# Two-layer fp32 encoder trunk on one core: FFN activations and x turned in 32x32 squares on VectorE and regrouped through scratch in device memory

## The chip, the cores and the metric

The kernel runs on one core of a Trainium2 chip. The core has five engines with a queue of instructions each: TensorE (PE; its weight loads are shown as PEld), VectorE (DVE), ScalarE (ACT), GpSimd (POOL) and SyncE (SP), and 16 DMA engines that move data between HBM and the core's own memory, SBUF. TensorE sums into PSUM. The metric is the device time of one execution in microseconds; the runs before have a median of 2511.64 us.

## The reference, cut to what matters

```python
for i in range(2):
    h = rms_norm(x, norm_mix_g[i])
    x = x + (retention_na_mixer if i == 0 else diff_attention_mixer)(h, ...)
    m = rms_norm(mem, norm_mem_g[i])
    x = x + memory_cross_attention(rms_norm(x, norm_xattn_g[i]), m, w_xq[i], w_xkv[i], w_xo[i], ...)
    x = x + swiglu_ffn(rms_norm(x, norm_ffn_g[i]), w_ffn_in[i], w_ffn_out[i])

def swiglu_ffn(h, w_in, w_out):
    g, u = jnp.split(h @ w_in, 2, axis=-1)
    return (jax.nn.silu(g) * u) @ w_out
```

x is 256 tokens x 2048 features, the FFN's hidden width is 5632, and everything is fp32.

## The kernel before

The 256 tokens are two tiles `t` of 128 rows; x stays in SBUF as `x_sb`, tokens on partitions. Every product with a weight matrix goes through `gemm`: the activation, features on partitions, is the stationary operand, the weight streams. Each fp32 number is held as two fp32r numbers, `hi` (a rounding copy) and `lo` (the remainder), and a product is three matmuls: hi x wh (L311), hi x wl (L312), lo x wh (L313).

Weights come in blocks of 512 x 512 fp32, 1 MB, into `raw` (three buffers) by SP's queue (L275). A block is used in two **units** of 256 rows. For a unit `prepare` has ScalarE cast `wh` (L285) and VectorE subtract `wl` (L286), three buffers each; `LOOK = 2` keeps two units prepared ahead, so the cast for unit n + 3 takes the buffer that unit n's matmuls read. A unit is 12 matmuls: three products, two rows of 128 features, two token tiles. There are 864 units. A block of 512 output columns sums over its units in two PSUM accumulators `acc` and ends with its epilogue.

The order of weights is a plan: per layer the mixer's input and output projections, the memory's key projection, xq, the memory's value projection, xo (the cross-attention's output projection), then the FFN in three groups of 4, 4 and 3 hidden blocks. For each group the gate and up columns are computed (`ffn_in`, two column blocks of eight units for each hidden block), and the group's part of the down product (`ffn_out`) follows. `woven` starts two column blocks of a phase on the features that are ready first and adds the last features later.

Work beside the matmuls is written as generators that a `Side` object steps once per unit. Each becomes instructions at that place in the program, and every engine runs its own instructions in that order.

What a matmul needs as stationary operand must stand with features on partitions, while x and the gated FFN activation `sg` stand with tokens there. `turn` (L335) turns 128x128 squares on TensorE by a matmul with the identity, four to a PSUM tile `pt`. `feed` uses it for the norms' inputs: two calls per 512 columns of `x_sb`, from which `gained` makes hi on ScalarE with the norm's gain (L340) and lo on VectorE (L341); the results are `hTx` for the cross-attention, `hTf` for the FFN and `hT` for the second layer's mixer. The norm's root over tokens is applied later, on the outputs: `finish_rstd` needs all four blocks' sums of squares and POOL's power. `act_T` does the same for the FFN's `sg`: two turns, then hi by `split` on ScalarE (L385) and lo on VectorE (L386), into `aT`. The queries and keys of the attention heads (`z`), retention's gate and the softmax tiles use `turn` or the like as well.

`add_x` (L697) adds a finished block to `x_sb`; L804 makes `sg` from the up accumulator.

Of the kernel before, what the change touches and what calls it, by code (L numbers as in the profile page):

```python
# [80 lines left out]
def trunk_kernel(  # L81
# [18 lines left out]
    qk = pool("qk", 1)  # L100
    vp = pool("vp", 2)
# [52 lines left out]
    def gain(i, layer, k):  # L154
        c = i * 32 + layer * 16 + k
        return gcol[:, c:c + 1]
# [58 lines left out]
    side = Side()  # L215
# [24 lines left out]
    for layer in range(2):  # L240
        j = layer // 2
# [10 lines left out]
        for g0, g1 in FFN_GROUPS:  # L252
            n = 2 * (g1 - g0)
# [72 lines left out]
    def square_sum(dst, src):  # L326
        junk = sqp.tile([P, NB], F32, tag="sq", name="junk")
        nc.scalar.activation(junk, src, AF.Square, accum_out=dst)

    def turn(srcs, u):  # L330
        pt = ps_t.tile([P, 2, T], F32, tag="pt", name="pt")
        for j in range(2):
            for t in range(2):
                c = (2 * u + j) * P
                nc.tensor.transpose(pt[:, j, t * P:(t + 1) * P], srcs[t][:, c:c + P], ident)  # L335
        return pt

    def gained(dst, kt, src, g):
        hi, lo = dst[0][:, kt], dst[1][:, kt]
        nc.scalar.activation(hi, src, AF.Copy, scale=g)  # L340
        nc.vector.scalar_tensor_tensor(out=lo, in0=src, scalar=g, in1=hi.bitcast(F32),  # L341
                                       op0=ALU.mult, op1=ALU.subtract)
# [20 lines left out]
    def finished(tasks):  # L363
        tasks = list(tasks)
        return lambda: all(t["done"] for t in tasks)

    def feed(dst, b, u, srcs, gi, layer, ssr, then=None):
        pt = turn(srcs, u)
        for j in range(2):
            k = 4 * b + 2 * u + j  # L370
            gained(dst, k, pt[:, j], gain(gi, layer, k))
        square_sum(ssr[0][:, u, b:b + 1], srcs[u])
        if then:
            then()
        return
        yield

    def feed_x(dst, b, gi, layer, ssr, wait=0):

        then = (lambda: finish_rstd(ssr)) if b == 3 else None  # L380
        t0 = side.add(feed(dst, b, 0, x_block(b), gi, layer, ssr), wait)
        return [t0, side.add(feed(dst, b, 1, x_block(b), gi, layer, ssr, then), wait + 1, finished([t0]))]

    def split(hi, lo, src):
        nc.scalar.copy(hi, src)  # L385
        nc.vector.tensor_sub(lo, src, hi)  # L386
# [299 lines left out]
    def finish_rstd(ssr):  # L686
        ss, rstd, r2 = ssr
        nc.vector.tensor_reduce(r2, ss, axis=AX.X, op=ALU.add)
        rsqrt_mean(rstd, r2, D)
        nc.vector.tensor_mul(r2, rstd, rstd)  # L690

    def x_block(b):
        return [x_sb[:, t, b * NB:(b + 1) * NB] for t in range(2)]
# [7 lines left out]
    hT = pair(which[0], "hT")  # L701
    ssr = new_ss("ssx")
# [12 lines left out]
    for layer in range(2):  # L715
        j = layer // 2
        A, B = which
        oT = pair(B, "oT")
        if layer % 2 == 0:
            gate = retention_na(j, hT, ssr[1:], oT, gate)  # L720
            kts = (8, 12, 0, 4)
        else:
            nc.vector.scalar_tensor_tensor(out=tabs, in0=tdiff, scalar=-1.0, in1=tdiff, op0=ALU.mult, op1=ALU.max)
            gate = diff_attention(j, hT, ssr[1:], oT, gate)
            kts = KT4

        mT = pair(A, "mT")
        m_v = mem[0].rearrange("(t p) d -> p t d", p=P)

        def mem_block(b):  # L730
            if layer == 0:
                mb = [att.tile([P, NB], F32, tag="att", name="mb") for _ in range(2)]
                for t in range(2):
                    nc.sync.dma_start(mb[t], m_v[:, t, b * NB:(b + 1) * NB])
            mts = [att.tile([P, 2, T], F32, tag="att", name="mt") for _ in range(2)]
            for u in range(2):
                nc.sync.dma_start(mts[u], mem_t[:, 4 * b + 2 * u:4 * b + 2 * u + 2])
            yield 2
            for u in range(2):
                feed_turned(mT, 2 * b + u, mts[u], 2, layer)  # L740
                yield 1
            if layer == 0:
                if b == 3:
                    side.drain(mtasks[:3])
                yield from block_sums(mb, b, mssr)

        mtasks = [side.add(mem_block(b)) for b in range(4)]

        gemm(kts, oT, lambda b, acc: add_x(acc, b), gate=gate)
        side.drain(mtasks)  # L750
        hT = pair(B, "hTx")
        ssr = new_ss("ssx")
        tasks = [t for b in range(4) for t in feed_x(hT, b, 1, layer, ssr, 1 if b == 3 else 0)]

        g = {"wait": 3}

        def epi_k(b, acc):
            g["k"], g["tk"] = normed_T(acc, mssr[1:], c_xk + layer, "kT")

        def epi_q(b, acc):  # L760
            g["q"], g["tq"] = normed_T(acc, ssr[1:], c_xq + layer, "qT")

        def epi_v(b, acc):
            g["v"] = tokens(acc, mssr[1:])

        gemm(KT4, mT, epi_k)
        gemm(KT4, hT, epi_q, gate=by_unit(tasks))
        xo = m8.tile([P, 2, 4, T], F32R, tag="m8", name="xo")
        xo = (xo[:, 0], xo[:, 1])
        heads = [side.add(attend(g, h, xo, h), cond=prepared(g)) for h in range(4)]  # L770
        gemm(KT4, mT, epi_v, steps=2)
        hT = pair(B, "hTf")
        ssr = new_ss("ssx")
        tasks = []

        def epi_xo(b, acc):
            add_x(acc, b)
            tasks.extend(feed_x(hT, b, 3, layer, ssr, 2))

        gemm((0,), xo, epi_xo, gate={0: heads[:2], 1: heads[2:]}, steps=2)  # L780
        gate = by_unit(tasks)

        def act_T(aT, zs, kt):
            for u in range(2):
                pt = turn(zs, u)
                split(aT[0][:, kt + 2 * u:kt + 2 * u + 2], aT[1][:, kt + 2 * u:kt + 2 * u + 2], pt)
                if u == 0:
                    yield 0

        for g0, g1 in FFN_GROUPS:  # L790
            aT = pair(A, "aT")
            n = g1 - g0
            sgs, atasks = {}, []

            def epi_in(i, acc):
                blk = i // 2
                r1 = ssr[1]
                if i % 2 == 0:
                    sgs[blk] = [zp.tile([P, NB], F32, tag="z", name="sg") for _ in range(2)]
                    for t in range(2):  # L800
                        nc.scalar.activation(sgs[blk][t], acc[t], AF.Silu, scale=r1[:, t:t + 1])
                    return
                for t in range(2):
                    nc.vector.scalar_tensor_tensor(out=sgs[blk][t], in0=acc[t], scalar=r1[:, t:t + 1],  # L804
                                                   in1=sgs[blk][t], op0=ALU.mult, op1=ALU.mult)
                atasks.append(side.add(act_T(aT, sgs[blk], 4 * blk), 2))

            gemm(KT4, hT, epi_in, gate=gate)
            gate = None
            kts = tuple(4 * b for b in range(n))  # L810
            last = g1 == 11
            side.drain(atasks[:-1])
            if last and layer == 0:
                hN = pair(B, "hT")
                ssn = new_ss("ssx")
                tasks = []

            def epi_out(b, acc):
                add_x(acc, b)
                if last and layer == 0:  # L820
                    tasks.extend(feed_x(hN, b, 0, 1, ssn, 1))
                elif last:
                    for t, xb in enumerate(x_block(b)):
                        nc.scalar.dma_start(out[0][t * P:(t + 1) * P, b * NB:(b + 1) * NB], xb)

            gemm(kts, aT, epi_out, gate={2 * n - 2: atasks[-1:]})
        if layer == 0:
            hT, ssr = hN, ssn
            gate = by_unit(tasks)
        which = which[::-1]  # L830
# [34 lines left out]
```

## Time and profile before

| what | value |
|---|---|
| three runs, median (range) | 2511.64 us (2511.25 to 2511.86) |
| the profiled execution, its own time | 2511.57 us |
| its span in the trace | 2509.8 us |
| TensorE busy | 2493.7 us, 99% |
| VectorE, ScalarE busy | 1427.0 us (57%), 1187.0 us (47%) |
| POOL busy | 50.6 us (2%) |
| HBM read, written | 465.91 MB, 2.10 MB |
| share of TensorE in the chain that ended last | 97% |

The span is the stretch that the trace covers. Matmuls are pipelined: the duration of one is longer than its distance to the next, so a stream is measured from start to start. The chain is followed back from the last instruction to whatever released it; an engine with a high share of busy time matters only where the chain runs through it. In a row of a timeline the bracket at the end is the idle time of the engine just before, and what ended it.

### The profile page before, as it was taken

How to read it: one execution, taken by the hardware profiler on the slowest of the kernel's cores; microseconds unless marked ns; L12 is line 12 of the kernel's file. 1: busy time of each engine (PE TensorE's matmuls, PEld its weight loads, DVE VectorE, ACT ScalarE, POOL GpSimd, SP SyncE). 2: the span in 40 equal slices, each digit the busy share in tenths (PEclk: the TensorE clock that was granted, in tenths of full speed). 3: DMA queues.
4: the chain of work that ended last, by engine and by line, in shares of the span. 5: the costliest groups of instructions: out<-in, count | busy, mean ns of one | idle time of the engine just before them, and what ended most of it. 6: DMA issues, size and time to landing. Idle time of an engine off the chain costs nothing.

```text
span 2509.8 us, 28710 instructions
## 1 busy us (share of the span) xinstructions
PE 2493.7 (99%) x11504; PEld 2067.5 (82%) x11504; DVE 1427.0 (57%) x1681; ACT 1187.0 (47%) x1538; POOL 50.6 (2%) x55
## 2 busy tenths in 40 slices
PE   8999999999999999999999999999999999999999
PEld 6888888888888888888888888888888888888887
DVE  6775565674545445544557766757654545455454
ACT  5554464564443444344445555645544444443443
POOL 1000000000000000000000000000000000000000
PEclk9999999999999999999999999999999999999999
DMA  8545566545555555555555555554555655556554
GB/s 285 183 159 182 186 220 200 168 163 190 186 189 195 188 197 185 190 196 185 185 185 167 168 169 179 199 190 155 183 184 188 197 186 196 189 185 200 186 189 163
DMA packets 236742, 469.87 MB, mean 187 GB/s; under 512 B 8128, under 2 KB 8768, under 8 KB 236608
## 3 DMA queue, kind: packets, MB, share of 16 engines
q1 hardware_dynamic: 233808, 463.50, 55.9%
q0 software_dynamic: 640, 2.10, 0.4%
q10 hardware_dynamic: 2160, 2.44, 0.3%
q8 instruction: 90, 1.47, 0.2%
q14 instruction: 44, 0.36, 0.0%
HBM read 465.91 MB, written 2.10 MB: 186 GB/s over the span
## 4 chain that ended last, share of the span: by engine, by line
PE 97%; DMA 1%; DVE 1%; ACT 0%; issue 0%; POOL 0%; ACTq 0%; DVEq 0%; POOLq 0%
PE acc L311 31%; PE acc L313 31%; PE acc L312 31%; PE pt L335 2%; DMA x_sb<-in_x 1%; PE pt L501 0%; PE pa_s L393 0%; PE pa_s L392 0%; PE pa_s L391 0%; PE pa_r L551 0%; DVE wl L286 0%; DMA dec<-in_ret_decay_bwd 0%; DMA lrow<-in_lambda_k 0%; PE pa_o L393 0%; PE pa_o L392 0%
## 5 line engine op out<-in xcount | busy, mean ns | idle before, releaser
L286 DVE TENSOR_TENSOR wl<-raw,wh 128x1024 fp32r<-128x1024 f32 (+1 forms) x865 | 1056.5, 1223 | 954.3 <-ACT wh L285 953.7
L285 ACT CAST wh<-raw 128x1024 fp32r<-128x1024 f32 (+1 forms) x865 | 910.3, 1052 | 1190.7 <-PE acc L313 1162.7
L311 PE MATMUL acc<-wh,hTfh 128*128 128x512 f32 x1408 | 551.5, 392 | 0.0
L313 PE MATMUL acc<-wh,hTfl 128*128 128x512 f32 x1408 | 548.5, 390 | 0.0
L312 PE MATMUL acc<-wl,hTfh 128*128 128x512 f32 x1408 | 547.9, 389 | 0.0
L311 PE MATMUL acc<-wh,hTh 128*128 128x512 f32 x832 | 331.9, 399 | 9.7 <-ACT wh L285 8.2
L312 PE MATMUL acc<-wl,hTh 128*128 128x512 f32 x832 | 325.6, 391 | 1.4 <-DVE wl L286 1.4
L313 PE MATMUL acc<-wh,hTl 128*128 128x512 f32 x832 | 325.6, 391 | 0.0
L313 PEld LDWEIGHTS acc<-wh,hTfl 128*128 128x128 f32 x1408 | 264.2, 188 | 55.6
L312 PEld LDWEIGHTS acc<-wl,hTfh 128*128 128x128 f32 x1408 | 264.4, 188 | 54.0
L311 PEld LDWEIGHTS acc<-wh,hTfh 128*128 128x128 f32 x1408 | 264.4, 188 | 53.8
L311 PE MATMUL acc<-wh,aTh 128*128 128x512 f32 x704 | 275.5, 391 | 0.0
L313 PE MATMUL acc<-wh,aTl 128*128 128x512 f32 x704 | 274.5, 390 | 0.0
L312 PE MATMUL acc<-wl,aTh 128*128 128x512 f32 x704 | 274.1, 389 | 0.0
L311 PEld LDWEIGHTS acc<-wh,hTh 128*128 128x128 f32 x832 | 156.9, 189 | 39.7 <-ACT wh L285 8.2
L313 PEld LDWEIGHTS acc<-wh,hTl 128*128 128x128 f32 x832 | 156.6, 188 | 33.8
L312 PEld LDWEIGHTS acc<-wl,hTh 128*128 128x128 f32 x832 | 157.0, 189 | 32.2 <-DVE wl L286 2.9
L313 PEld LDWEIGHTS acc<-wh,aTl 128*128 128x128 f32 x704 | 132.2, 188 | 27.7
L312 PEld LDWEIGHTS acc<-wl,aTh 128*128 128x128 f32 x704 | 132.2, 188 | 26.8
L311 PEld LDWEIGHTS acc<-wh,aTh 128*128 128x128 f32 x704 | 132.2, 188 | 26.9
L311 PE MATMUL acc<-wh,oTh 128*128 128x512 f32 x256 | 100.2, 391 | 0.0
L313 PE MATMUL acc<-wh,oTl 128*128 128x512 f32 x256 | 99.7, 390 | 0.0
(184 smaller groups left out, 1875.8 us busy)
## 6 DMA issues: line engine op xcount, KB each, us to landing
raw<-in_w_ffn_in SPq DMA_DIRECT2D x176, 1024.0 KB, 5.1
raw<-in_w_ffn_out SPq DMA_DIRECT2D x88, 1024.0 KB, 5.1
raw<-in_w_in_ab SPq DMA_DIRECT2D x55, 1024.0 KB, 5.2
raw<-in_w_in_c SPq DMA_DIRECT2D x48, 1024.0 KB, 5.2
raw<-in_w_out_ab SPq DMA_DIRECT2D x16, 1024.0 KB, 5.2
raw<-in_w_xkv SPq DMA_DIRECT2D x16, 1024.0 KB, 5.0
raw<-in_w_out_c SPq DMA_DIRECT2D x16, 1024.0 KB, 5.1
raw<-in_w_xq SPq DMA_DIRECT2D x8, 1024.0 KB, 5.2
```

Source lines behind the costliest of these rows:

```text
L285: nc.scalar.copy(wh[:, js], raw[:, rs])
L286: nc.vector.tensor_sub(wl[:, js], raw[:, rs], wh[:, js])
L311: nc.tensor.matmul(acc[t], lhsT=hi[:, kt, ts], rhs=wh[:, j], start=first and j == 0, stop=False)
L312: nc.tensor.matmul(acc[t], lhsT=hi[:, kt, ts], rhs=wl[:, j], start=False, stop=False)
L313: nc.tensor.matmul(acc[t], lhsT=lo[:, kt, ts], rhs=wh[:, j], start=False, stop=last and j == 1)
L335: nc.tensor.transpose(pt[:, j, t * P:(t + 1) * P], srcs[t][:, c:c + P], ident)
```

## The change

The turns of `x_sb` (for `hTx`, `hTf` and the second layer's `hT`) and of the FFN's `sg` leave TensorE. The new `regroup` takes both token tiles of a 512-column block: VectorE's transpose turns all 32x32 squares within their 32 partitions, one instruction per token tile, into a buffer `zt`; SP's queue writes the 512 KB to scratch in HBM (`zd`, four buffers); four loads on POOL's queue, one for each group of 32 features, bring the squares to the partitions that they belong to (`zT`). Five units later (`MOVE`) ScalarE and VectorE make hi and lo from `zT`, now from SBUF: in `feed` ScalarE four times 128x256 and VectorE eight times 128x128, in `act_T` two each over 128x4x128. The buffers are those of the heads' values (`vp`), of queries and keys (`qk`) and the single `m8`. `feed_x` adds one task instead of two.

```diff
+MOVE = 5
+    dram = pool("dram", 4, space=bass.MemoryType.DRAM)
-    def feed(dst, b, u, srcs, gi, layer, ssr, then=None):
-        pt = turn(srcs, u)
-        for j in range(2):
-            k = 4 * b + 2 * u + j
-            gained(dst, k, pt[:, j], gain(gi, layer, k))
-        square_sum(ssr[0][:, u, b:b + 1], srcs[u])
...
+    def regroup(srcs, room=""):
...
+        zt = zt.rearrange("p (j k t b) -> p j k t b", j=4, k=4, t=2)
+        for t in range(2):
+            nc.vector.transpose(zt[:, :, :, t], srcs[t].rearrange("p (k j a) -> p j k a", j=4, a=32))
+        zd = dram.tile([4, 32, 4, T], F32, name="zd")
+        nc.sync.dma_start(zd.rearrange("i a j n -> (i a) (j n)"), zt.rearrange("p j k t b -> p (j k t b)"))
+        for j in range(4):
+            nc.gpsimd.dma_start(zT[32 * j:32 * j + 32].rearrange("a (i n) -> a i n", i=4),
+                                zd[:, :, j].rearrange("i a n -> a i n"))
+        return zT.rearrange("p (i k t b) -> p i k t b", i=4, k=4, t=2)
+
+    def feed(dst, b, srcs, gi, layer, ssr, room):
+        zT = regroup(srcs, room)
+        for t in range(2):
+            square_sum(ssr[0][:, t, b:b + 1], srcs[t])
+        if b == 3:
+            finish_rstd(ssr)
+        yield MOVE
+        for k in range(4):
...
+            nc.scalar.activation(hi, src, AF.Copy, scale=g)
+            for t in range(2):
+                nc.vector.scalar_tensor_tensor(out=lo[:, t], in0=src[:, t], scalar=g, in1=hi[:, t].bitcast(F32),
+                                               op0=ALU.mult, op1=ALU.subtract)
...
         def act_T(aT, zs, kt):
-            for u in range(2):
-                pt = turn(zs, u)
-                split(aT[0][:, kt + 2 * u:kt + 2 * u + 2], aT[1][:, kt + 2 * u:kt + 2 * u + 2], pt)
-                if u == 0:
-                    yield 0
+            zT = regroup(zs)
+            yield MOVE
+            for t in range(2):
+                split(*(x[:, kt:kt + 4, t * P:(t + 1) * P].rearrange("p k (i b) -> p k i b", i=4) for x in aT),
+                      zT[:, :, :, t].rearrange("p i k b -> p k i b"))
...
-                atasks.append(side.add(act_T(aT, sgs[blk], 4 * blk), 2))
+                atasks.append(side.add(act_T(aT, sgs[blk], 4 * blk)))
```

The change moves instructions. Lines of the new kernel have other numbers: L287 is the cast, L288 the remainder, L313 to L315 the three matmuls, L381 the transpose, L383 the write, L385 the loads, L400 and L402 hi and lo of a feed, L411 the remainder of `act_T`, L722 the add to x, L829 the gate product. The numbers in the names count tiles; in the rows of the first two places they tell the units apart.

ScalarE where xo ends and the FFN begins, layer 0. Before: feeds 0 and 1 (`pt_4400`, then `pt_4431` and `pt_4442`) and the casts around them; `wh_4486` belongs to the first FFN unit:

```order
L285 CAST wh_4382<-raw_4362 128x1024
...
L340 ACTIVATE hTfh_4285<-pt_4400,gcol_104 128x256
L285 CAST wh_4415<-raw_4413 128x1024
L340 ACTIVATE hTfh_4285<-pt_4400,gcol_104 128x256
...
L285 CAST wh_4453<-raw_4413 128x1024
L340 ACTIVATE hTfh_4285<-pt_4431,gcol_104 128x256
L340 ACTIVATE hTfh_4285<-pt_4442,gcol_104 128x256
...
L285 CAST wh_4486<-raw_4484 128x1024
```

And now: the FFN's units 1 to 6 are `wh_4501`, `4517`, `4571`, `4599`, `4617` and `4645`, and the feeds 0, 1 and 2 are `zz_4400`, `zz_4432` and `zz_4484`:

```order
L287 CAST wh_4501<-raw_4499 128x1024
...
L287 CAST wh_4517<-raw_4499 128x1024
L287 CAST wh_4571<-raw_4569 128x1024
L400 ACTIVATE hTfh_4302<-zz_4400,gcol_106 128x256 x4
...
L287 CAST wh_4599<-raw_4569 128x1024
L287 CAST wh_4617<-raw_4615 128x1024
L400 ACTIVATE hTfh_4302<-zz_4432,gcol_106 128x256 x4
L287 CAST wh_4645<-raw_4615 128x1024
L400 ACTIVATE hTfh_4302<-zz_4484,gcol_106 128x256 x4
```

The copies of feed 0 have moved from before the first FFN unit's cast to behind that of unit 3, those of feed 1 behind that of unit 5.

VectorE at the same place, now: the adds of xo's last block (`acc0_4497`, `acc1_4498`), block 3's transposes (`zz_4547`), and the remainders of feeds 0 and 1:

```order
L288 TENSOR_TENSOR wl_4518<-raw_4499,wh_4517 128x1024
L722 TENSOR_TENSOR x_sb_105<-acc0_4497,x_sb_105 128x512
L722 TENSOR_TENSOR x_sb_105<-acc1_4498,x_sb_105 128x512
L381 STREAM_TRANSPOSE zz_4547<-x_sb_105 128x16x32 x2
L402 SCALAR_TENSOR_TENSOR hTfl_4303<-zz_4400,gcol_106,hTfh_4302 128x128 x8
L713 TENSOR_REDUCE ssxq_4306<-ssx_4304 128x2
L288 TENSOR_TENSOR wl_4572<-raw_4569,wh_4571 128x1024
L322 TENSOR_SCALAR ssxr_4305<-ssxq_4306 128x2
L288 TENSOR_TENSOR wl_4600<-raw_4569,wh_4599 128x1024
L288 TENSOR_TENSOR wl_4618<-raw_4615,wh_4617 128x1024
L402 SCALAR_TENSOR_TENSOR hTfl_4303<-zz_4432,gcol_106,hTfh_4302 128x128 x8
```

Feed 0's remainders stand behind the adds and transposes of xo's last block, and feed 1's behind the `wl` of unit 5. TensorE's matmuls of the first FFN unit are written in this order now:

```order
L315 MATMUL acc1_4498<-wh_4465,xo_4037 128x512
L313 MATMUL acc0_4567<-wh_4501,hTfh_4302 128x512
L314 MATMUL acc0_4567<-wl_4502,hTfh_4302 128x512
L313 MATMUL acc1_4568<-wh_4501,hTfh_4302 128x512
L314 MATMUL acc1_4568<-wl_4502,hTfh_4302 128x512
L315 MATMUL acc0_4567<-wh_4501,hTfl_4303 128x512
```

The first matmul that reads `hTfl` has become the fifth of its unit, where it was the third; unit 3, the first that reads feed 1, is written alike.

VectorE in a steady FFN block, before and then now; a `wl` is one unit:

```order
L804 SCALAR_TENSOR_TENSOR sg<-acc_4674,ssxr,sg 128x512
L804 SCALAR_TENSOR_TENSOR sg<-acc_4675,ssxr,sg 128x512
L286 TENSOR_TENSOR wl<-raw,wh 128x1024 x2
L386 TENSOR_TENSOR aTl<-pt,aTh 128x512
L286 TENSOR_TENSOR wl<-raw,wh 128x1024
```

```order
L829 SCALAR_TENSOR_TENSOR sg<-acc_4707,ssxr,sg 128x512
L829 SCALAR_TENSOR_TENSOR sg<-acc_4708,ssxr,sg 128x512
L381 STREAM_TRANSPOSE zz<-sg 128x16x32 x2
L288 TENSOR_TENSOR wl<-raw,wh 128x1024 x6
L411 TENSOR_TENSOR aTl<-zz,aTh 128x4x128 x2
L288 TENSOR_TENSOR wl<-raw,wh 128x1024 x10
```

Two transposes have come in behind the gate products, and `aTl` has moved from two and three units behind to six.

## Rows read from the trace of the kernel before

**Rows 1.** The page: span; busy time by engine; the chain by engine and line.

```profile
span 2509.8 us, 28710 instructions
PE 2493.7 (99%) x11504; PEld 2067.5 (82%) x11504; DVE 1427.0 (57%) x1681; ACT 1187.0 (47%) x1538; POOL 50.6 (2%) x55
...
PE 97%; DMA 1%; DVE 1%; ACT 0%; issue 0%; POOL 0%; ACTq 0%; DVEq 0%; POOLq 0%
PE acc L311 31%; PE acc L313 31%; PE acc L312 31%; PE pt L335 2%; DMA x_sb<-in_x 1%; PE pt L501 0%; PE pa_s L393 0%; PE pa_s L392 0%; PE pa_s L391 0%; PE pa_r L551 0%; DVE wl L286 0%; DMA dec<-in_ret_decay_bwd 0%; DMA lrow<-in_lambda_k 0%; PE pa_o L393 0%; PE pa_o L392 0%
```

**Rows 2.** Waits, whole span: us in total, times, longest.

```profile
ACT wh L285 <- PE acc L313: 1162.7, 737, 2.6
DVE wl L286 <- ACT wh L285: 953.7, 737, 2.6
```

**Rows 3.** Windows: length, busy PE PEld DVE ACT POOL, clock, DMA share, GB/s.

```profile
86.00:88.00 2.00, 2.00 (x12) 1.68 (x11) 1.96 (x6) 2.00 (x6) 1.85 (x4) 1.00 1.01 316
96.00:98.00 2.00, 1.06 (x8) 0.75 (x7) 2.00 (x4) 1.04 (x1) 0.00 (x0) 1.00 0.08 29
594.00:727.00 133.00, 133.00 (x600) 110.06 (x599) 65.91 (x60) 57.35 (x60) 0.00 (x0) 1.00 0.58 190
```

**Rows 4.** Groups of instructions by line and shape: busy us, mean ns | idle.

```profile
L335 PE MATMUL pt<-ident,sg 128*128 128x128 f32 x192 | 28.7, 272 | 0.0
L335 PE MATMUL pt<-ident,x_sb 128*128 128x128 f32 x160 | 24.9, 274 | 0.0
```

**Rows 5.** Timeline of ScalarE: start, us, instruction, idle before and its end.

```profile
627.90 1.06 ACT L285 CAST wh<-raw 128x1024 fp32r<-128x1024 f32 x1 [1.66 <-PE acc L313]
630.62 1.06 ACT L285 CAST wh<-raw 128x1024 fp32r<-128x1024 f32 x1 [1.66 <-PE acc L313]
```

**Rows 6.** Timeline of TensorE, two sets of turns.

```profile
641.30 0.60 PE L335 MATMUL pt<-ident,sg 128*128 128x128 f32 x4
...
644.51 0.60 PE L335 MATMUL pt<-ident,sg 128*128 128x128 f32 x4
```

**Rows 7.** TensorE: timeline at the FFN's start; then tile aTh, first use 727.6.

```profile
549.45 0.48 PE L311 MATMUL acc<-wh,hTfh 128*128 128x512 f32 x1
...
L311 PE MATMUL acc<-wh,aTh x704: 387/389/481, 727.6 to 2504.9; 128*128 128x512 f32 x176
```

**Rows 8.** Timeline of VectorE at the end of an FFN block.

```profile
593.79 1.40 DVE L804 SCALAR_TENSOR_TENSOR sg<-acc,ssxr,sg 128x512 f32<-128x512 f32 x2
595.37 1.23 DVE L286 TENSOR_TENSOR wl<-raw,wh 128x1024 fp32r<-128x1024 f32 x1 [0.17 <-ACT wh L285]
```

**Rows 9.** Groups of instructions by line and shape, ScalarE and VectorE.

```profile
L697 DVE TENSOR_TENSOR x_sb<-acc,x_sb 128x512 f32<-128x512 f32 x80 | 52.0, 683 | 8.1 <-PE acc L313 8.1
L385 ACT CAST aTh<-pt 128x512 fp32r<-128x512 f32 x44 | 25.5, 579 | 0.0
L341 DVE SCALAR_TENSOR_TENSOR hTfl<-pt,gcol,hTfh 128x256 fp32r<-128x256 f32 x32 | 14.3, 477 | 0.0
L340 ACT ACTIVATE hTfh<-pt,gcol 128x256 fp32r<-128x256 f32 x32 | 13.8, 468 | 1.9 <-DVE hTfl L341 1.9
```

**Rows 10.** DMA: tiles bias (whole span) and out; the page's row of raw.

```profile
L533 POOL DMA_DIRECT2D bias<-in_na_rpb x8: 619/619/797, 16.7 to 87.2; - x8
DMA to landing us min/median/max: 5.0/7.2/10.8
...
L824 ACTq DMA_DIRECT2D out<-x_sb x8: 338/338/353, 2467.9 to 2506.5; - x8
DMA to landing us min/median/max: 2.1/4.4/7.9
...
raw<-in_w_ffn_in SPq DMA_DIRECT2D x176, 1024.0 KB, 5.1
```

**Rows 11.** Tile bias again, in the stretch 80 to 100 us.

```profile
L533 POOL DMA_DIRECT2D bias<-in_na_rpb x4: 619/619/658, 85.3 to 87.2; - x4
```

**Rows 12.** Timeline of VectorE where xo ends.

```profile
549.09 1.28 DVE L697 TENSOR_TENSOR x_sb<-acc,x_sb 128x512 f32<-128x512 f32 x2
```

More of the change, by code (lines that the diff above doesn't have):

```diff
@@ L365, in finished @@
         return lambda: all(t["done"] for t in tasks)
-    def feed(dst, b, u, srcs, gi, layer, ssr, then=None):
-        pt = turn(srcs, u)
-        for j in range(2):
-            k = 4 * b + 2 * u + j
-            gained(dst, k, pt[:, j], gain(gi, layer, k))
-        square_sum(ssr[0][:, u, b:b + 1], srcs[u])
[L373 to L382, printed above, removed]
+    def regroup(srcs, room=""):
+        if room == "m8":
+            both = m8.tile([P, 2, 4 * T], F32, tag="m8", name="zz")
+            zt, zT = both[:, 0], both[:, 1]
+        elif room:
+            zt, zT = (qk.tile([P, 4 * T], F32, tag=room + x, name="zz") for x in "hl")
+        else:
+            zt, zT = (vp.tile([P, 4 * T], F32, tag="v" + x, name="zz") for x in "hl")
+        zt = zt.rearrange("p (j k t b) -> p j k t b", j=4, k=4, t=2)
[7 more added lines that the diff above has]
+        return zT.rearrange("p (i k t b) -> p i k t b", i=4, k=4, t=2)
@@ new lines, in feed @@
+    def feed(dst, b, srcs, gi, layer, ssr, room):
[6 more added lines that the diff above has]
+        for k in range(4):
+            g = gain(gi, layer, 4 * b + k)
+            hi, lo = (x[:, 4 * b + k].rearrange("p (t i b) -> p t i b", t=2, i=4) for x in dst)
+            src = zT[:, :, k].rearrange("p i t b -> p t i b")
+            nc.scalar.activation(hi, src, AF.Copy, scale=g)
+            for t in range(2):
+                nc.vector.scalar_tensor_tensor(out=lo[:, t], in0=src[:, t], scalar=g, in1=hi[:, t].bitcast(F32),
+                                               op0=ALU.mult, op1=ALU.subtract)
@@ L384, in split, with feed_x @@
+    def feed_x(dst, b, gi, layer, ssr, room=""):
+        return [side.add(feed(dst, b, x_block(b), gi, layer, ssr, room))] * 2
     def split(hi, lo, src):
@@ L752, in trunk_kernel @@
         ssr = new_ss("ssx")
-        tasks = [t for b in range(4) for t in feed_x(hT, b, 1, layer, ssr, 1 if b == 3 else 0)]
+        tasks = [t for b in range(4) for t in feed_x(hT, b, 1, layer, ssr, ("", "", "qT", "m8")[b])]
         g = {"wait": 3}
@@ L777, in epi_xo @@
             add_x(acc, b)
-            tasks.extend(feed_x(hT, b, 3, layer, ssr, 2))
+            tasks.extend(feed_x(hT, b, 3, layer, ssr, ("", "", "qT", "kT")[b]))
         gemm((0,), xo, epi_xo, gate={0: heads[:2], 1: heads[2:]}, steps=2)
@@ L820, in epi_out @@
                 if last and layer == 0:
-                    tasks.extend(feed_x(hN, b, 0, 1, ssn, 1))
+                    tasks.extend(feed_x(hN, b, 0, 1, ssn))
                 elif last:
```

## The prediction, made before the changed kernel was run

> **What bounds the kernel now.** I read the share of busy time first, then the chain that ended last, then the waits. TensorE works in 99% of the span and carries 97% of the chain [rows 1]; nearly all of it are the three weight products, and the turns into `pt` at L335 are 2%. The waits say the same from the other side: ScalarE's cast of a weight tile waits for the matmuls that still read the buffer it is to fill, VectorE's remainder waits for the cast [rows 2]. So the two elementwise engines run behind TensorE with time to spare, and what leaves TensorE's list leaves the kernel's time, unless a new wait takes its place. The granted clock is 1.00, and it is still 1.00 in the stretch 96 to 98 us, where TensorE stood for nearly half of it [rows 3]; I put no price on the clock.
>
> **What is removed.** 160 turns of `x_sb` go, and 176 of the 192 that read `sg` (16 are retention's gate and stay): 336 turns, 84 sets of four [rows 4]. A turn's mean of 272 ns overlaps its neighbours, so I take what a set adds to the stream. One cast starts every 2.72 us in a stretch without turns [rows 5]: that is a unit of 12 matmuls, 0.227 us each. Two sets follow each other at 641.30 and 644.51, 3.21 us with one unit between [rows 6]: 3.21 - 2.72 = 0.49 us a set. A long stretch gives nearly the same: the first gate-and-up group lasts from 549.45 to 727.6 [rows 7], 178.1 us for 64 units (174.1) and eight sets (two of `x_sb`, two for each of three blocks), 0.51 us each. I take 0.49: 84 x 0.49 = **41.2 us off TensorE** (up to 42.5 by the long stretch).
>
> **What is added in a steady FFN block** (22 of these; the four feeds of the second layer's input projection stand the same way on ScalarE, 26 in all). Count from the end of the block's last matmul. VectorE's gate products take 1.40 us for two, beginning while the second half is still being summed, and are done about 1.0 after it [rows 8]. Then two transposes of 128x512. No row of before shows that operation. The nearest are VectorE's rows on a 128x512 tile: 683 ns alone, 1.28 us for two [rows 9, 12]; an operation of 256 elements takes 477 ns [rows 9], which bounds it below, and twice the long row, 2.6 us for two, bounds it above. I take 1.28, because that row reads and writes as many elements: done at +2.3. By the Trainium skill (VectorE: DVE Perf Modes, The three transpose paths) one 128x128 block of two-byte data takes 311 ns on VectorE, by which the two tiles, eight such blocks, would be an estimated 2.5 us and the whole sum about 2480 us; no row of before shows it.
>
> The round trip R runs from there: the write of 512 KB on SP's queue, then four reads of 128 KB on POOL's. For the write the rows are stores of 256 KB, 2.1 to 7.9 us with a median of 4.4, and weight loads of 1 MB at 5.1: I take 4.5. Four issues on POOL at 0.62 are 2.5 us, and the last one's landing starts after three of them, 1.9. The bias loads, 256 KB each on this same queue, land in 5.0 to 10.8 with a median of 7.2 [rows 10]. At half that size I take 4.0, below the shortest row. R = 4.5 + 1.9 + 4.0 + 0.2 of handing over = 10.6 us; from the smallest, with half the shortest landing, 2.1 + 1.9 + 2.5 = 6.5, from the largest 7.9 + 1.9 + 10.8 + 0.2 = 20.8.
>
> How much R is free: the order puts ScalarE's copy out of `zT` behind the cast of the eighth unit ahead, and unit nine starts 8 x 2.72 = 21.8 us after the block's end. Between arrival and that unit lie two copies at 0.58, a cast of 1.05 and a remainder of 1.22 [rows 5, 8, 9], 3.5 us with the hand-overs. So data that arrive by 18.2, that is R up to 18.2 - 2.3 = 15.9 us, cost TensorE **nothing**; the estimate leaves 5 us of cover. Beyond it each us costs one us per block, 26 in all.
>
> SP's write waits for the transposes at +2.3 and holds the weight load behind it, but that load's buffer comes free only with the next remainder but one, near +5; a weight block issued then is wanted four units later (10.9 us) and lands in 5.1. Over 42 regroupings 44 MB come on top of 470; DMA's share goes from 0.58 [rows 3] to some 0.64. POOL's power for the norm queues behind reads that wait for the write, but is due only when the first gate block ends, 14 units (38 us) on. VectorE's eight 128-wide remainders in place of four 256-wide ones, and ScalarE reading SBUF, lie beside matmuls. Cost of all this: 0, or up to 0.5 us per layer in the cross-attention's key phase, where VectorE is fullest.
>
> **What is added where attention ends and the FFN begins** (two layers). Here the cover is gone. Before, both halves of feed 0 were copied before the first FFN unit. Now the order has feed 0's `hTfh` behind the cast for FFN unit 3, whose buffer is read by the last attention unit until its end, E. Cast to E + 1.1, first copy 0.47 [rows 9]: first FFN matmul at +1.6. TensorE has four matmuls without the remainder ahead, so the first that wants `hTfl` could run at +0.9 without a wait, and at +2.5 with this one. On VectorE the same row of work is: two adds to x, the second only after E, done at +0.9; block 3's two transposes, +2.1; then the first 128-wide remainder. From 683 ns for 512 and 477 for 256 it is 0.37: +2.5. Both paths meet: stop 1 is **1.6 us**. Feed 1 stands behind the cast for unit 5, which waits for the end of unit 2; its remainders stand behind that unit's `wl` too: 0.1 + 1.05 + 1.22 + 0.4 = 2.8 against 0.9, stop 2 is **1.9 us**. Feeds 2 and 3 are due one and seven units after their copies can run: 0. Before, TensorE had no stop here: L311 starts at 549.45 straight after a set of turns, with the adds still under way until 550.37 [rows 7, 12]. Sum 3.5 us a layer, **7.0 for two**. Feed 0's second transpose follows an add at the end of block 1's first half, six matmuls and four units before E: -12.2 + 0.7 + 0.7 + 0.3 of slack for VectorE's queue = 10.5 us before E, so R over 11.6 adds to stop 1; the estimate of 10.6 just passes.
>
> **Sum.** Against the profiled execution, 2511.57 us with a span of 2509.8 [rows 1] and 0.07 below the median of the runs: 2511.6 - 41.2 + 7.0 = **2477 us**.
>
> **The rivals.**
> A, the forecast, 2472 to 2486: the upper end holds R of 14 (2 x 2.4), the key phase (1.0) and transposes twice as long (2 x 1.3).
> B, the stops are smaller, since copies start sooner than the order and the buffers say: 2470 to 2472. Against it: casts wait for matmuls 737 times [rows 2].
> C, **the round trip comes late; slower than before.** Its place is ScalarE's copy from `zT`, with the next cast behind it. At R = 16.8 the loss is 26 x 0.9 + 2 x 5.2 = 34 us, and the saving is spent; above that the kernel is slower, by 28 us for each us, up to 2477 + 26 x 4.9 + 2 x 9.2 = 2623 us at R = 20.8. For it: the slow ends of two rows added [rows 10]. Against it: the bias loads shared DMA engines at full share [rows 3], and a read here has half their size.
> D, VectorE's and SP's queues slip, so that a weight block is late: with half a us at each of 42 regroupings 2498. Against it: DMA's share of 0.58 and VectorE's of half [rows 3].
> E, the change does not give TensorE its slots back because something else sets the pace of a unit: about 2511. Against it: a cast waits 1.66 of each 2.72 us for TensorE [rows 5].
> F, POOL's issues are held up while VectorE works. If each waited for one remainder of 1.22 us, R would be 13.0 and the time 2480, within A. Against a longer wait: in 86 to 88 us VectorE is busy 1.96 of 2.00, and POOL's four issues there take 0.62 to 0.66 [rows 3, 11]. If, however, each were held for the two or three VectorE operations that can follow one another here, 3.1 us, R would be 4.5 + 12.4 + 4.0 + 0.2 = 21.1 and the time 2477 + 26 x 5.2 + 2 x 9.5 = 2631. The Trainium skill (SBUF — State Buffer, SBUF: two separate sides) warns of this case: a DMA issued by GpSimd has its descriptors written by that engine, VectorE can lock it out of the port, and 620 ns became 3100; it names two-port modes and not subtractions of two tensors (Who interferes with whom). By that exception the trace agrees, at 0.62.
>
> **How the numbers follow.** Chances: A 0.67, B 0.04, C 0.11 (0.07 of it slower than before, 0.03 between 2486 and 2501), D 0.09, E 0.05, F's long wait 0.04. From 2469 to 2501 lie A, B, nearly all of D and a part of C: 0.81. A difference of 0.2%, 5 us, is about what can be told from none here: faster 0.83, same 0.06, slower 0.11.
>
> **What would show it.** Turns at L335 down to 176, none from `x_sb`. In the windows of the FFN groups TensorE's pitch is 12 matmuls per 2.72 us without gaps; the casts still wait for L313. In the waits one new entry, the matmuls on `hTfh` or `hTfl` waiting for VectorE or ScalarE, about 1.6 and 1.9 us, four in all. The reads land by 10.6 us after the transposes. It would be wrong if ScalarE waits for DMA at its copies from `zz`, if the transposes take several us, or if weight loads on SP's queue wait for the write.

## The result and the profile after

The changed kernel takes 2487.94 us (2487.04 to 2492.25, four runs) against 2511.44 of before in the same comparison: a ratio of 0.991, 95% interval 0.9893 to 0.9927, 23.5 us less. The forecast was 2477, so the direction held and the gain fell short by 11 us. The profiled execution is the longest of the four, 2492.25 us with a span of 2490.3; its own difference to before is 19.3 us, and the accounts below are made against that.

The page of the new kernel: busy time by engine, the chain by engine and by line, and two rows of DMA issues (KB each, median us to landing).

```profile
PE 2459.9 (99%) x11168; PEld 2038.3 (82%) x11168; DVE 1480.4 (59%) x1845; ACT 1188.5 (48%) x1538; POOL 144.4 (6%) x223
...
PE 94%; DMA 3%; DVE 2%; issue 0%; ACT 0%; POOL 0%; ACTq 0%; POOLq 0%; DVEq 0%
PE acc L313 30%; PE acc L314 30%; PE acc L315 30%; DMA zd<-zz 1%; DMA zz<-zd 1%; PE pt L337 1%; DVE wl L288 1%; DMA raw<-in_w_in_ab 1%; DVE x_sb L722 0%; PE pt L526 0%; PE pa_s L418 0%; PE pa_s L417 0%; PE pa_s L416 0%; PE pa_r L576 0%; DVE zz L381 0%
...
zd<-zz SPq DMA_DIRECT2D x42, 512.0 KB, 3.7
zz<-zd POOLq DMA_DIRECT2D x168, 128.0 KB, 4.9
```

336 of TensorE's instructions are gone (x11504 to x11168), as planned. But the chain, 97% TensorE before [rows 1], is 94% now, and the write and the reads of the scratch stand in it. Where DMA is in the chain, TensorE has waited for it. TensorE's share of busy time, 99% in both, does not show this; the waits do (us in total, times, longest):

```profile
PE acc L313 <- ACT hTfh L400: 11.8, 6, 2.6
PE acc L314 <- DVE wl L288: 3.9, 3, 2.9
ACT hTfh L400 <- DMA zz<-zd: 7.6, 3, 3.5
ACT hTh L400 <- DMA zz<-zd: 3.9, 1, 3.9
```

Six stops where four were forecast, and ScalarE waiting for the loads, which was named as a sign that the forecast is wrong. TensorE's timeline has the stops with their places, the first three in layer 0 where xo ends (the bracket is the idle time ahead):

```profile
545.19 0.80 PE L313 MATMUL acc<-wh,hTfh 128*128 128x512 f32 x1 [2.64 <-ACT hTfh L400]
...
553.95 0.50 PE L313 MATMUL acc<-wh,hTfh 128*128 128x512 f32 x1 [1.54 <-ACT hTfh L400]
562.01 0.79 PE L313 MATMUL acc<-wh,hTfh 128*128 128x512 f32 x1 [2.11 <-ACT hTfh L400]
...
1263.41 0.50 PE L314 MATMUL acc<-wl,aTh 128*128 128x512 f32 x1 [2.94 <-DVE wl L288]
```

These are FFN units 1, 3 and 5, and one stop in the last down product of layer 0, where the second layer's hT is fed. Layer 1 has units 1, 3 and 5 again, at 1761.58, 1768.86 and 1777.19. From the start of one matmul to the next, less the usual 0.23, the seven cost 2.80, 1.71, 2.28, 3.10, 1.71, 1.71 and 2.54, 15.9 us together.

The windows show what else was lost (length, busy PE, PEld, DVE, ACT, POOL, granted clock, share of DMA, GB/s):

```profile
594.00:727.00 133.00, 133.00 (x589) 110.12 (x588) 71.74 (x69) 58.49 (x61) 6.56 (x12) 1.00 0.65 216
532.00:562.00 30.00, 23.71 (x95) 18.28 (x93) 21.43 (x39) 15.88 (x30) 10.36 (x17) 0.94 0.95 287
...
545.00:548.00 3.00, 2.81 (x7) 2.23 (x8) 2.45 (x10) 2.67 (x8) 0.00 (x0) 0.50 1.03 317
548.50:552.00 3.50, 3.50 (x17) 2.88 (x16) 1.80 (x3) 1.05 (x1) 0.00 (x0) 1.00 1.02 355
```

The steady group (first row) has no gap and its DMA share is 0.65, where 0.64 was expected and 0.58 measured before [rows 3]. Where xo ends (second row) the DMA share is 0.95. And behind the stop at 545 the granted clock is 0.50, the lower level of 1.2 GHz, for some 3 us; then it is back at 1.00. The first FFN group of layer 0 is 7.69 us longer than 64 units of 2.72; its two stops inside account for 3.99, which leaves 3.7. Counted from start to start over the eight slow matmuls, the two dips (behind units 1 and 5) cost 1.6 and 1.7; most of the rest is TensorE's weight loads waiting for `hTfl` behind the stop at unit 3. Layer 1 has one dip, behind its longest stop: 1.7 of the 2.2 that are left there.

From first matmul to first matmul, the stages that changed (us):

| stage | before | after | what it holds |
|---|---|---|---|
| memory's keys, layer 0 | 25.53 | 21.76 | 8 sets gone |
| xo, layer 0 | 26.56 | 26.58 | sets gone, stop at unit 1 come |
| first gate and up group, layer 0 | 178.11 | 181.77 | 8 sets gone, two stops, two dips |
| first down product | 88.02 | 87.04 | 2 sets gone |
| second gate and up group | 177.00 | 174.08 | 6 sets gone |
| last down product, layer 0 | 69.30 | 68.56 | 8 sets gone, one stop |
| first gate and up group, layer 1 | 178.09 | 180.53 | 8 sets gone, two stops, one dip |

The second gate and up group is 64 x 2.72 to the hundredth: the steady blocks give back 0.49 us a set in full. Stops are 15.9 us, dips 5.0, the waits for `hTfl` 0.7 and smaller ones some 0.4, 22.0 us together; with the 19.3 us gained that is 41.3, against 41.2 forecast for the removal. No larger loss is left to find.

### The profile page after: what moved, and what is told of

Same layout as the page of the kernel before. It is cut to its first block, busy times and chain, and to the rows that moved or that the text cites. A ratio compares the mean times of both kernels' runs of the same rounds, so it can differ in the third digit from the quotient of the medians.

```text
span 2490.3 us, 28635 instructions
## 1 busy us (share of the span) xinstructions
PE 2459.9 (99%) x11168; PEld 2038.3 (82%) x11168; DVE 1480.4 (59%) x1845; ACT 1188.5 (48%) x1538; POOL 144.4 (6%) x223
## 3 DMA queue, kind: packets, MB, share of 16 engines
q10 hardware_dynamic: 2160, 2.44, 0.3%
## 4 chain that ended last, share of the span: by engine, by line
PE 94%; DMA 3%; DVE 2%; issue 0%; ACT 0%; POOL 0%; ACTq 0%; POOLq 0%; DVEq 0%
PE acc L313 30%; PE acc L314 30%; PE acc L315 30%; DMA zd<-zz 1%; DMA zz<-zd 1%; PE pt L337 1%; DVE wl L288 1%; DMA raw<-in_w_in_ab 1%; DVE x_sb L722 0%; PE pt L526 0%; PE pa_s L418 0%; PE pa_s L417 0%; PE pa_s L416 0%; PE pa_r L576 0%; DVE zz L381 0%
## 5 line engine op out<-in xcount | busy, mean ns | idle before, releaser
L288 DVE TENSOR_TENSOR wl<-raw,wh 128x1024 fp32r<-128x1024 f32 (+1 forms) x865 | 1054.4, 1221 | 881.6 <-ACT wh L287 881.3
L287 ACT CAST wh<-raw 128x1024 fp32r<-128x1024 f32 (+1 forms) x865 | 909.6, 1052 | 1177.8 <-PE acc L315 1153.1
L313 PE MATMUL acc<-wh,hTfh 128*128 128x512 f32 x1408 | 550.8, 391 | 11.8 <-ACT hTfh L400 11.8
L315 PE MATMUL acc<-wh,hTfl 128*128 128x512 f32 x1408 | 548.6, 390 | 0.0
L313 PE MATMUL acc<-wh,hTh 128*128 128x512 f32 x832 | 331.8, 399 | 9.6 <-ACT wh L287 8.1
L315 PE MATMUL acc<-wh,hTl 128*128 128x512 f32 x832 | 325.5, 391 | 0.0
L313 PEld LDWEIGHTS acc<-wh,hTfh 128*128 128x128 f32 x1408 | 265.4, 189 | 69.2 <-ACT hTfh L400 14.3
L315 PEld LDWEIGHTS acc<-wh,hTfl 128*128 128x128 f32 x1408 | 265.4, 189 | 56.1 <-DVE hTfl L402 0.7
L315 PE MATMUL acc<-wh,aTl 128*128 128x512 f32 x704 | 273.9, 389 | 0.0
L313 PE MATMUL acc<-wh,aTh 128*128 128x512 f32 x704 | 273.9, 389 | 0.0
L313 PEld LDWEIGHTS acc<-wh,hTh 128*128 128x128 f32 x832 | 156.9, 189 | 39.8 <-ACT wh L287 8.1
L315 PEld LDWEIGHTS acc<-wh,hTl 128*128 128x128 f32 x832 | 156.6, 188 | 33.9
L385 POOL DMA_DIRECT2D zz<-zd x168 | 91.7, 553 | 1553.7 <-DMA zd<-zz 1450.3
L313 PEld LDWEIGHTS acc<-wh,aTh 128*128 128x128 f32 x704 | 132.1, 188 | 27.5
L315 PEld LDWEIGHTS acc<-wh,aTl 128*128 128x128 f32 x704 | 132.1, 188 | 27.4
L313 PE MATMUL acc<-wh,oTh 128*128 128x512 f32 x256 | 100.2, 392 | 0.0
```

What stands on the lines that cost most here:

```text
L287: nc.scalar.copy(wh[:, js], raw[:, rs])
L288: nc.vector.tensor_sub(wl[:, js], raw[:, rs], wh[:, js])
L313: nc.tensor.matmul(acc[t], lhsT=hi[:, kt, ts], rhs=wh[:, j], start=first and j == 0, stop=False)
L315: nc.tensor.matmul(acc[t], lhsT=lo[:, kt, ts], rhs=wh[:, j], start=False, stop=last and j == 1)
L385: nc.gpsimd.dma_start(zT[32 * j:32 * j + 32].rearrange("a (i n) -> a i n", i=4), zd[:, :, j].rearrange("i a n -> a i n"))
```

## Why the trips were late where xo ends: the trace

First a steady block, the timelines of VectorE, SP, POOL and ScalarE in turn:

```profile
597.43 1.30 DVE L381 STREAM_TRANSPOSE zz<-sg 128x512 f32<-128x512 f32 x2
598.75 0.34 SPq L383 DMA_DIRECT2D zd<-zz  x1
602.96 2.21 POOL L385 DMA_DIRECT2D zz<-zd  x4 [42.85 <-DMA zd<-zz]
611.15 1.14 ACT L410 CAST aTh<-zz 128x512 fp32r<-128x512 f32 x2
```

Transposes end at 598.73, the write goes out at once, the reads 4.2 us later, the last at 604.6. In the stretch 590 to 815 the reads' median landing is 4.6, so R is 604.6 + 4.6 - 598.73 = 10.5 us. ScalarE takes the data at 611.15, straight behind a cast and without a wait.

Then the third feed where xo ends, layer 0, the same four engines:

```profile
538.03 1.30 DVE L381 STREAM_TRANSPOSE zz<-x_sb 128x512 f32<-128x512 f32 x2
539.36 0.34 SPq L383 DMA_DIRECT2D zd<-zz  x1
552.46 2.18 POOL L385 DMA_DIRECT2D zz<-zd  x4 [9.56 <-DMA zd<-zz]
561.45 1.71 ACT L400 ACTIVATE hTfh<-zz,gcol 128x256 fp32r<-128x256 f32 x4 [3.18 <-DMA zz<-zd]
```

13.1 us from the write's issue to the reads (this write alone took 12.5 us to land), and R is 561.45 - 539.33 = 22.1. The DMA view of 520 to 570 us says why, median landing in the last column:

```profile
raw<-in_w_ffn_in SPq DMA_DIRECT2D x7, 1024.0 KB, 7.6
zd<-zz SPq DMA_DIRECT2D x4, 512.0 KB, 8.3
zz<-zd POOLq DMA_DIRECT2D x16, 128.0 KB, 6.8
```

In the kernel before, seven loads of `raw` in that stretch landed in 5.0. Four trips begin within some 13 us here, 4 MB written and read while the weights go on. The weights themselves are slower, which makes the engines' bandwidth the suspect; that POOL or SP serves its queue in order is the rival.

## The experiments

**1. The FFN activation alone.** `feed` turns x on TensorE as before, with its old waits; `act_T` stays as changed.

```diff
-        return [side.add(feed(dst, b, x_block(b), gi, layer, ssr, room))] * 2
...
+        t0 = side.add(feed_turn(dst, b, 0, x_block(b), gi, layer, ssr), wait)
+        return [t0, side.add(feed_turn(dst, b, 1, x_block(b), gi, layer, ssr, then), wait + 1, finished([t0]))]
```

> Part alone: only the FFN activation (act_T) goes through scratch; x is turned on TensorE as before, in all three feeds. 44 sets of turns leave TensorE. Theory (the whole loss stands at the feeds of x, nothing in the steady FFN blocks): 2511.4 - 44 x 0.49 = 2490 us, no new stop of TensorE, and ScalarE's copies from zz wait for nothing. Rival (the loss is spread over all 42 round trips): 22 of 42 parts of the 17.6 us that are missing in the changed kernel, so 2499 us.

Measured: 2491.09 us (ratio 0.9917, 0.9900 to 0.9934), 20.8 us less for 44 sets, 0.47 each. Its waits have no entry of a matmul on `aTh`; the group 594 to 727 is full:

```profile
594.00:727.00 133.00, 133.00 (x588) 110.13 (x587) 71.70 (x69) 58.53 (x61) 6.58 (x12) 1.00 0.67 217
```

The steady blocks pay nothing for their 22 trips. One ScalarE copy of the 22 did wait, 1.6 us, for its loads (R 14.1), which the expectation excluded; no matmul waited behind it. The rival is out.

**2. The feeds of x alone.** `act_T` turns on TensorE as before, `feed` stays as changed.

```diff
-            zT = regroup(zs)
-            yield MOVE
...
+            for u in range(2):
+                pt = turn(zs, u)
...
```

> The other part alone: only x goes through scratch (hTx, hTf and the second layer's hT), the FFN activation is turned on TensorE. 40 sets leave TensorE, 19.6 us. Theory (the loss stands at the feeds): the 17.6 us are lost here in full, 2511.4 - 19.6 + 17.6 = 2509 us, no difference that can be told, with stops of TensorE at FFN units 1, 3 and 5 and the granted clock down to 0.50 behind the longer ones. Rival (loss spread over round trips): 2511.4 - 19.6 + 8.4 = 2500 us.

Measured: 2507.54 us (ten runs, 2504.0 to 2509.85; 0.9983, 0.9973 to 0.9992): 40 sets are off TensorE and 4 us are left of them. So some 15 us stand at the feeds. The stops are at units 1 and 3 in both layers, at unit 5 in layer 1 alone, and one of 1.7 us near the end of layer 0. The waits of this kernel:

```profile
PE acc L313 <- ACT hTfh L400: 10.5, 5, 3.6
```

**3. The changed kernel with half the weight traffic in three stretches.** For the blocks of xo and the first 16 FFN units in both layers, and for the last down product of layer 0 and the 16 units behind it, the second half of each weight block is left out and both of its units use the first, so part of the products is made with other weights:

```diff
+            if thin(at["unit"]):
+                halves.add((i, b, c))
+                nc.sync.dma_start(raw[:, 0:2], src[:, 0:2])
...
+            r = 0 if (i, b, c) in halves else 2 * h
```

> The changed kernel, but in three stretches (from the start of xo to the 16th FFN unit in both layers; from the last down product of layer 0 to the 16th unit of the next input projection) only the first half of each weight block is loaded, and its two units both use that half: 0.5 MB a block in place of 1 MB, so that part of the products there is computed with other weights; instructions and their order are the same otherwise. Theory (the round trips are late there because four of them and the weight stream together fill the DMA engines): R falls towards the 10.5 us of the steady blocks, the stops at unit 5 and at the end of layer 0 go, stop 1 comes down to 1.7, the clock stays at 1.00; what stays is the four stops by ScalarE's order, 4 x 1.7: 2511.4 - 41.2 + 6.8 = 2477 us. Rival (POOL's queue, which waits for one write after another and has four loads to issue, makes them late): traffic does not matter, 2486 to 2488 us with the same stops.

Measured: 2479.05 us (0.9871, 0.9856 to 0.9886), 8.9 us under the changed kernel with the same 84 trips. TensorE's wait, and the DMA view of 520 to 570 us:

```profile
PE acc L327 <- ACT hTfh L414: 6.4, 4, 1.8
...
raw<-in_w_ffn_in SPq DMA_DIRECT2D x7, 512.0 KB, 3.7
zd<-zz SPq DMA_DIRECT2D x4, 512.0 KB, 4.7
zz<-zd POOLq DMA_DIRECT2D x16, 128.0 KB, 5.7
```

The write's median landing falls from 8.3 to 4.7 us (the third one's from 12.5 to 8.3), and the share of DMA in 532 to 562 us from 0.95 to 0.80. Both stops at unit 5 and the one near the end of layer 0 are gone. What stays is four stops at units 1 and 3, 1.54 to 1.79 idle: the forecast's four. In the profiled execution, 2479.93 us, a dip stayed behind the longest of them in layer 0 (its group is 3.84 us over its units, 1.71 of it the stop at unit 3). The other three, at 2479.0 to 2479.1 with a mean clock of 1.000 against its 0.999, are 2 us over the expected 2477 too; at 0.475 us a set and 7.1 us for the four stops from start to start, 2479 is what one would expect. The order of instructions on ScalarE, VectorE, POOL and SP is that of the changed kernel, so the weight traffic is what made the trips late. Whether it did so on the shared engines or by standing ahead on SP's queue is asked in experiment 8.

**4. MOVE at 2.**

```diff
-MOVE = 5
+MOVE = 2
```

> The changed kernel with MOVE at 2 in place of 5: ScalarE's copies stand three units earlier, behind the cast of unit 5 ahead in a steady FFN block. Theory (the cover of a round trip is set by where the copies stand on ScalarE, R free up to 15.9 - 3 x 2.72 = 7.7 us, and R is 10.5 in the steady blocks of the changed kernel): 2.8 us lost in each of 22 blocks, 62 us, so 2488 + 62 = 2550 us, more if the clock falls in the stops, with ScalarE waiting for the loads at aTh. Rival (matmuls wait only for data that they read themselves, and these are due 8 units or more later): about 2488 us.

Measured: 2492.7 us, a single run. My theory's 2550 fell, but not in the way that its rival says either, since the edit did not do what I took it to do. VectorE's and ScalarE's timelines in a steady block:

```profile
637.72 1.29 DVE L381 STREAM_TRANSPOSE zz<-sg 128x512 f32<-128x512 f32 x2
...
651.44 1.14 ACT L410 CAST aTh<-zz 128x512 fp32r<-128x512 f32 x2
```

651.44 - 639.01 = 12.4 us behind the transposes, as in the changed kernel (611.15 - 598.73 = 12.4), and with the same six remainders between. The copies do not move with `MOVE` there. It was said ahead of the prediction that every engine runs its instructions in the order in which the generators make them; here it does not. But for one remainder, the edit moved work only around the cross-attention's keys and queries: hTx's fourth feed is late there, with a stop of 1.54 us on `wl` in each layer. For the feeds of hTf the order is the changed kernel's, and yet the stops differ (2.99 and none at units 1 and 5 of layer 0, 2.44 and 0.70 in layer 1): how late a trip comes there varies by a microsecond or more. The limit of 15.9 us for R was not reached in a steady block of any run; the longest there, 14.1 in experiment 1 and 14.2 in experiment 6, cost no stop.

**5. The two kinds of feed with stops turned on TensorE.** hTf and the second layer's hT by `feed_turn`, hTx and `act_T` through scratch.

> hTf (the FFN's input) and the second layer's hT are turned on TensorE as before; hTx and the FFN activation go through scratch: 60 of the 84 sets leave TensorE. Theory (all loss stands at the eight feeds of hTf and the four of the second layer's hT): 2511.5 - 60 x 0.485 = 2482 us, and no stop of TensorE but those of the kernel before. Rival (hTx loses as well, where VectorE is fullest and four trips come within a few units): 1 to 3 us a layer more, 2484 to 2488 us.

Measured: 2482.93 us (0.9883, 0.9869 to 0.9898), 0.48 us for each of 60 sets. The rival, a loss at hTx, is out: with its four trips the key phase lasts 21.76 us, eight units to the hundredth, in the changed kernel too.

**6. Three feeds on TensorE.** Feeds 0 to 2 of hTf by `feed_turn`; for the second layer's hT other buffers, and a longer delay before the copies of the first two feeds.

```diff
-            tasks.extend(feed_x(hT, b, 3, layer, ssr, ("", "", "qT", "kT")[b]))
+            tasks.extend(feed_x(hT, b, 3, layer, ssr, ("", "", "qT", "kT")[b], 2 if b in (0, 1, 2) else None))
...
-                    tasks.extend(feed_x(hN, b, 0, 1, ssn))
+                    tasks.extend(feed_x(hN, b, 0, 1, ssn, ("qT", "kT", "", "")[b], None, (8, 8, 5, 5)[b]))
```

> Only the first three feeds of hTf in each layer are turned on TensorE; feed 3, the four feeds of the second layer's hT, hTx and the FFN activation go through scratch. Feeds 0 and 1 of that hT use the buffers of queries and keys and are copied eight units after their transposes in place of five. 72 sets leave TensorE. Theory: one round trip at a time shares DMA with the weights where xo ends, feed 3 is due only with unit 13 and hT's feeds 0 and 1 twelve units on, so no stop: 2511.5 - 72 x 0.485 = 2476.5 us, under both kernels. Rival (copies behind a late trip hold the next cast wherever trips come close): the stop of 3 us near the end of layer 0 stays and the clock falls behind it, 2480 to 2482 us.

Measured: 2477.53 us (0.9862, 0.9847 to 0.9876), 34.2 us under before and 10.4 under the changed kernel. TensorE's matmuls have no wait for `hTfh` or `hTfl`, and where xo ends the stretch is full, at 0.60 of DMA:

```profile
528.00:562.00 34.00, 34.00 (x163) 28.14 (x163) 25.00 (x39) 22.72 (x44) 3.79 (x5) 1.00 0.60 197
```

ScalarE at feed 1 of the second layer's hT:

```profile
1249.63 1.31 ACT L400 ACTIVATE hTh<-zz,gcol 128x256 fp32r<-128x256 f32 x3 [3.94 <-DMA zz<-zd]
```

The longer delay did not move the copies here either: those of feeds 0 and 1 begin 12.9 and 16.6 us behind their transposes (12.8 and 16.6 in the changed kernel), and feed 1's wait for the loads is as long as it was. Still, the stop on `wl` is 0.20 us in place of 2.94: the next cast now stands ahead of the feed's last copy, and the `wl` ahead of its remainders. So a late copy costs what is ordered behind it. What in the edit changed that order was not separated.

**7. Two feeds on TensorE.** The same with `b in (0, 1)`: feeds 2 and 3 share the stretch.

> As the kernel with the first three feeds of hTf turned on TensorE, but only the first two are; feeds 2 and 3 go through scratch, two round trips within three units where xo ends. 76 sets leave TensorE. If two trips there still come in time (R under 13 us for feed 2, due with unit 5): 2511.5 - 76 x 0.485 = 2474.6 us. If the weights loaded at the same time make feed 2 late as in the changed kernel (2.3 and 2.5 us at unit 5, 1.6 us of low clock behind each): 2482 us, worse than with three feeds on TensorE.

Measured: 2477.56 us (0.9864, 0.9848 to 0.9881): neither number. Two trips pass without a stop at unit 5, but feed 3 is late enough for ScalarE to wait, the cast behind it is late, and small stops on `wl` take back most of what the four sets more gave (1.9 us). Its window, ScalarE's timeline and TensorE's wait:

```profile
528.00:562.00 34.00, 34.00 (x159) 28.20 (x158) 26.47 (x43) 21.35 (x39) 5.18 (x9) 1.00 0.72 227
...
563.50 1.71 ACT L400 ACTIVATE hTfh<-zz,gcol 128x256 fp32r<-128x256 f32 x4 [3.60 <-DMA zz<-zd]
...
PE acc L314 <- DVE wl L288: 2.1, 5, 0.8
```

**8. The write on POOL's queue.**

```diff
-        nc.sync.dma_start(zd.rearrange("i a j n -> (i a) (j n)"), zt.rearrange("p j k t b -> p (j k t b)"))
+        nc.gpsimd.dma_start(zd.rearrange("i a j n -> (i a) (j n)"), zt.rearrange("p j k t b -> p (j k t b)"))
```

> The changed kernel, with the write to scratch issued on POOL's queue in place of SP's, all 42; the traffic is the same, and ScalarE's order changes by one cast here and there. What is asked: is the write late where xo ends because it stands on the same queue as the 1 MB weight loads ahead of it (13.1 us from its issue to the loads that wait for it at 539.36), or because the weight stream, writes and reads together fill the 16 DMA engines whatever the queue? Queue order: the write lands in 3 to 5 us there, the stops at FFN unit 5 and the one near the end of layer 0 go, 2479 us as with half the weights. Shared engines: the stops at unit 5 stay, with ScalarE waiting for zz there, 2485 to 2490 us.

Measured: 2502.68 us (0.9962, 0.9948 to 0.9976), 15 us slower than the changed kernel and outside both numbers. On the question asked, the DMA view of 520 to 570 us:

```profile
zd<-zz POOLq DMA_DIRECT2D x4, 512.0 KB, 7.7
zz<-zd POOLq DMA_DIRECT2D x16, 128.0 KB, 7.2
```

Away from the weights' queue the write still needs a median of 7.7 us there (8.3 on it), the third and fourth 9.9 and 10.3 (12.5 and 11.1), at a DMA share of 0.93 in 532 to 562 us. So a place behind the weights on SP's queue is not needed for a late write; what the place behind POOL's own reads adds to it now was not separated. What I left out is POOL's own order: the third feed's write now waits behind the second's reads, and goes out 4.0 us after its transposes.

```profile
543.84 0.56 POOL L383 DMA_DIRECT2D zd<-zz  x1
...
PE acc L313 <- ACT wh L287: 12.0, 4, 8.5
PE acc L313 <- ACT hTfh L400: 11.8, 4, 4.5
```

The stops at unit 1 are 4.49 and 4.25 us now, and casts have become late as well (three of the four waits on `wh`; the one of 8.5 us is the kernel's start, 8.1 in the changed kernel). The granted clock is 0.50 in 20 us of this profile, where it was in 10 of the changed kernel's. How much of the 15 us is POOL's order and how much ScalarE's, which changed by a cast in places, was not separated.

## Why the prediction was right, and where it was not

**The removal** held: 41.2 us forecast, 41.3 found by adding up the profiled execution. Over medians a set is worth 0.47 to 0.48 (experiments 1, 5 and 6), a little under the 0.49 taken from one pair.

**The transposes** held: 1.29 to 1.30 us for two, 1.28 taken.

```profile
L381 DVE STREAM_TRANSPOSE zz<-sg 128x512 f32<-128x512 f32 x44 | 28.5, 687 | 0.0
L381 DVE STREAM_TRANSPOSE zz<-x_sb 128x512 f32<-128x512 f32 x40 | 27.0, 694 | 0.1
```

The nearest row, any VectorE operation on a 128x512 tile [rows 9], was the right price. By the Trainium skill (VectorE: DVE Perf Modes, The three transpose paths) it would have been an estimated 2.5 us; the measurement decides, and it is half.

**The steady blocks** held: R 10.5 against 10.6, hidden, cost 0.

**Stops at units 1 and 3** held in kind and size where data were in time: 1.71 us each (2.0 at unit 3 with the waits for `hTfl` behind it), against 1.6 and 1.9. Experiment 3 leaves just these.

**The first step that failed** is "Feeds 2 and 3 are due one and seven units after their copies can run: 0", with R taken as 10.6 "just" passing for feed 0. I had the limit of feed 0, 11.6 us, and a range of R to 20.8, but took one R for the whole kernel, and DMA's share as an average of 0.64. In the 30 us where four trips meet the share is 0.95, R of feed 0 is 12.9 in layer 0 and that of feed 2 is 22.1. Measured in place of 0: 2.28 and 2.54 at unit 5, and 1.1 more at unit 1 of layer 0.

**The second** is the four feeds of the second layer's hT "stand the same way on ScalarE" as the blocks: feeds 0 and 1 come within two units, feed 1's copy waits for DMA, and the cast behind it is late:

```profile
1257.10 1.71 ACT L400 ACTIVATE hTh<-zz,gcol 128x256 fp32r<-128x256 f32 x4 [3.93 <-DMA zz<-zd]
```

That is rival C's mechanism, at one place out of 26. R is 16.6 there, for which the prediction's limit of 15.9 would give 0.7 us; the stop cost 3.1, and 0.36 in experiment 6 with the same R in another order.

**The third** is "I put no price on the clock", from one window [rows 3]. It cost 5.0 us. The stop in that window was 0.94 us long; in the profile of experiment 1 it was 1.90 at the same place, and the clock fell behind it.

In short, 7.0 was the term that was mis-sized: 22.0 in the profiled execution, some 16 to 18 in the median (41.2, or 39.9 at 0.475 a set, less 23.5). The measured time lies above A, the forecast's own 2472 to 2486; it fell inside the range because C and D had kept its upper half open, and that is luck as far as the steps go.

**Rival F's long wait** did not come. 168 issues on POOL took 553 ns in the mean, while VectorE was busy 59% of the time. The lock-out that the Trainium skill describes (SBUF — State Buffer, SBUF: two separate sides) is not in this trace. That agrees with its part Who interferes with whom, which names VectorE's two-port modes for it, and operations with two SBUF inputs, as the subtractions here, only against GpSimd instructions that read SBUF.

## What to carry to other kernels

In this kernel a transfer was hidden or not by the share of DMA in its own 30 us, not by the kernel's average: before moving work to DMA, list where several round trips start together, and add their bytes to what streams there already. Where one round trip at a time leaves eight units of cover, take it; where several come at once and the data are due at the next unit, leave the work on TensorE. Then read from the trace where the copies really stand: a delay in a generator moved them in one phase and not in others. Here the mixture, six of the 42 blocks (three feeds of hTf in each layer) on TensorE and the rest through scratch, is the fastest kernel run, level with that of two feeds: 2477.5 and 2477.6 us.

## What the runs showed of the hardware

The granted clock fell to 0.50, the level of 1.2 GHz, for some 3 us behind stops of TensorE of 2.64, 2.11 and 2.38 us idle in the changed kernel, each time at a price of 1.6 to 1.7 us beside the stop; it stayed at 1.00 behind all three stops of 1.54. It also stayed at 1.00 behind the longest, 2.94 us, before which TensorE had worked without a gap as it had before the others:

```profile
1263.00:1267.00 4.00, 3.59 (x16) 2.94 (x17) 2.62 (x3) 1.41 (x2) 1.54 (x3) 1.00 0.63 201
```

The other profiles are as mixed: it fell behind 1.79 us in experiment 3, 1.90 in experiment 1 and 2.44 in experiment 4, and not behind 2.99 in experiment 4. So the length of a stop alone does not settle it; what else does is open. A stop of TensorE has two prices, and which one applies was seen here only by the window behind it.
